# A two-block fp32 network on one core: the pooling layer projects differences of grid rows, and the first modulation moves to TensorE

## The chip, the cores and the metric

One core of a Trainium2 chip runs the whole program as one launch. The metric is the device time of an execution in microseconds (us), as the median of several runs. Five engines work side by side, each through its own instructions in order: TensorE (PE in the profile, with its weight loads as PEld), VectorE (DVE), ScalarE (ACT), GpSimd (POOL) and SyncE (SP), which here only issues transfers. Transfers run on 16 DMA engines.

## The reference, cut to what matters

Two transformer-like blocks run over 256 tokens of width 2048, all in float32. The first block has an even layer and an odd layer.

In every layer a modulation vector comes from the condition: `silu(c) @ w_ada + b_ada`, split into shift, scale and gate. The even layer needs shift and scale for two conditions, `c` for the latent tokens and `c_ctx` for the context tokens. Its input is `u = x * (1 + scale) + shift`, which is projected by `w_in_e`; the first 2048 columns of that projection are the keys and values of both the 256 latent and the 256 context tokens.

The odd layer, here called the pooling layer, is

```
xp, gate = split(u @ w_in_o)                  # 2 x 2048 columns
xg = xp.reshape(4 rows, 64 columns, 2048)     # the 256 tokens are a grid
z  = [mean over a window of rows of g  -  g   for g, window in 4 groups of 512]
z  = (z @ w_pool[group]) * pool_scale
y  = (z * silu(gate)) @ w_out_o
```

The windows are 2, 4, 8 and 16 rows. With 4 rows the last two are the mean over all rows. `z` therefore depends only on differences between grid rows.

The second block holds a recurrent layer (rwkv7) with a bonus term `sum(r * k * r_k)` per head, attention, a cross attention to a memory of 256 tokens, and a feed-forward layer.

## The kernel before, in words

**Products.** Every large projection splits both operands into a high and a low part in a reduced format (`fp32r`) and adds three products: high by high, high by low, low by high. `mm3` (line 162) issues them. Activations stand transposed, 128 input columns by tokens, in tiles `h` and `l`; they are the stationary operand. Weights stream as the moving operand, 512 columns at a time. `load_w` (line 157) fetches two blocks of 128 rows by 512 columns (512 KB) into a `wr` tile, a ring of four, and `split_w` makes `wh` by a ScalarE copy (line 148) and `wl` by a subtraction (line 154), a ring of three each. `split_on` says which engines subtract: (V, G) means that VectorE takes one half and GpSimd the other.

**`project`** (line 182) runs over blocks of 512 output columns, and in each over pairs of 128-row blocks of the weight: one load, then 12 matmuls (two row blocks, two groups of 128 tokens, three products). After each such step it advances the background generator `bg` by `bgn_default` steps. `feed` is a generator advanced in the same places; it makes the input while it is being used.

**Opening.** First the cross attention's keys and values of the memory (`project(memT, ...)`, 16 steps). Behind it, the modulation for the first two blocks of 128 channels is made. Then the channels come in five parts, `PARTS = ((0,2),(2,2),(4,4),(8,4),(12,4))`. Each part transposes its channels of `x` and `ctx`, scales and shifts them (`store_affine`) by the modulation `mod0` of its own channels, and multiplies them with four column blocks of the weight (24 matmuls per load: 4 groups of 128 tokens, two row blocks, three products). The results of the parts are added up in SBUF (lines 528 to 534: ScalarE copies in the first part; in the next two VectorE adds the even ones, and ScalarE and GpSimd the odd ones; VectorE adds all of them later). While a part multiplies, `bg` makes the modulation of the next; `drain` ends it before the next part begins.

Modulation has two forms. `ada_block` streams `w_ada` through TensorE with the four columns `c4` (both conditions, high and low part) as stationary operand. `ada_block_v` multiplies rows of `w_ada` on VectorE (line 355, two conditions, one instruction for each block of 128 rows and condition), from tiles `ar`. In each part, kind 0 (shift) goes by the first and kind 1 (scale) by the second. Both end with small matmuls that bring the result into columns (`pm`): one or two moving columns each.

**Pooling layer** (phase b, lines 972 to 1068). `do_xp(g)` and `do_gate(g)` are projections of 512 columns each from `u1T` (8 steps each); `pool(g)` transposes `xp`, forms the window means minus itself on VectorE, and splits; `mix(g)` multiplies with `w_pool[g]` (2 steps), times `silu(gate)`, and transposes the result. `make_u1` makes `u1T` as the feed of the first projection. `bg` makes the layer's output gate (`ada_gate`: 16 transfers of 256 KB into `ar`, a ring of three, and one VectorE instruction each, line 379) and `affine_x1`, one step for each step of a projection.

**Bonus** (line 1276). Each of 8 pairs of a 128-channel block and a token group is a matmul with the products `qq` as stationary operand and two moving columns.

The program is put in order by a scheduler that starts from the order written and lets an instruction pass one that is not ready, so TensorE's order can differ a little from the text.

Of the kernel before, what the change touches and what calls it, by code (L numbers as in the profile page):

```python
# [17 lines left out]
D = 2048  # L18
# [36 lines left out]
def tile_kernel(ctx: ExitStack, tc: tile.TileContext, I: dict, out: bass.AP):  # L55
# [8 lines left out]
              "b": {"yt": (1024, 8), "h": (512, 8), "f": (512, 8), "gt": (512, 4), "ar": (512, 3), "aa": (512, 1)},  # L64
# [78 lines left out]
    split_on = [(V, G)]  # L143
# [37 lines left out]

    def project(x, w, c0, ncols, evac, korder=None, cw=512, w_k0=0, cbs=None, feed=None, lead=2, late=0, early=0):
# [10 lines left out]
        for cb in cbs:  # L193
# [3 lines left out]
            def products(k0, w, t):  # L197
                for q in range(2):
                    xh, xl = x.get(k0 + q, t)
                    mm3(acc[t][:, :n], xh, xl, w[0][:, q], w[1][:, q], k0 == korder[0] and q == 0,  # L200
                        k0 == korder[-1] and q == 1)
# [41 lines left out]
    def store_affine(x, kt, pt, scale, bias, ts=(0, 1), scratch="h"):  # L243

        full = tl(scratch, [128, 2, T], name="full")
# [8 lines left out]
    def affine_steps(x, src, scale, bias, scratch="h"):  # L254

        for ts, kts in (((0,), (0, 2)), ((1,), (0, 2)), ((0, 1), range(4, 16, 2))):
            for kt in kts:
                store_affine(x, kt, transpose2(src, kt, ts), scale, bias, ts, scratch)
                yield
# [57 lines left out]
    def ada_block(t0, nt, kind):  # L317
# [17 lines left out]
    def set_mod0(pm, t0, nt, kind):  # L335
        b = pr1[:, 32 + kind * 16 + t0:32 + kind * 16 + t0 + nt]
        V.scalar_tensor_tensor(mod0[:, t0:t0 + nt, kind, :], pm, float(kind),
                               b[:, :, None].to_broadcast([128, nt, 2]), op0=AL.add, op1=AL.add)

    def ada_block_v(t0, nt, kind):  # L340
# [17 lines left out]
        pm = pside([128, nt, 2], name="pm")  # L358
        for q in range(nt):
            for a in range(2):  # L360
                PE.matmul(pm[:, q, a:a + 1], acc[a][:, q * 128:(q + 1) * 128], ones[:, :1], start=True, stop=True)
        set_mod0(pm, t0, nt, kind)
# [20 lines left out]
    def ada_cols(l, kind, j):  # L383
        acc = yield from ada_acc(l, kind * D + j * 512)
        pm = pbg([128, 4])
        for q in range(4):
            PE.matmul(pm[:, q:q + 1], acc[:, q * 128:(q + 1) * 128], ones[:, :1], start=True, stop=True)
        c0 = 32 + l * 48 + kind * 16 + j * 4
        V.scalar_tensor_tensor(mod1[:, kind, j * 4:j * 4 + 4], pm, float(kind), pr1[:, c0:c0 + 4], op0=AL.add, op1=AL.add)
# [1456 lines left out]
```

## Time and profile before

| | |
|---|---|
| time, median of 3 runs | 2589.76 us (2586.3 to 2592.92) |
| profiled execution: its own time, its span | 2595.39 us, 2593.7 us |
| TensorE busy in the span | 2442.7 us (94%), 11551 matmuls |
| VectorE, ScalarE, GpSimd busy | 1813.7 us (70%), 1157.8 us (45%), 262.1 us (10%) |
| mean granted TensorE clock | 0.974 |
| transfers | 483.12 MB, mean 186 GB/s |

The opening runs from 0 to about 342 us of the span: the memory's keys and values to 79 us, and then the five parts, whose first matmuls come at 87, 124, 175, 237 and 294 us. The pooling layer begins at 894 us, when its first matmul is issued, and its last transposes end at 1127 us, already among the matmuls of the output projection. The two bonus sums lie at 1341 and 1551 us. A matmul is reported as a record with a modelled end, so neighbouring records overlap; the time that a matmul takes in a stream is read from the distance of the starts. Transposes and matmuls of plain float32 operands appear as two records each.

### The profile page before, as it was taken

The numbers are of one execution on the slowest core, as the hardware profiler recorded it, in microseconds if no ns is written. First come the engines' busy times: TensorE is split into PE (matmuls) and PEld (weight loads), VectorE is DVE, ScalarE is ACT, GpSimd is POOL, SyncE is SP. The second block draws the span as 40 slices with busy tenths as digits, with TensorE's granted clock in tenths as the row PEclk, the third lists the DMA queues.
The fourth block names the chain that finished last, engine by engine and source line by source line (L and its number), as shares of the span: only waits on it lengthen the run. The fifth ranks groups of instructions, "written<-read, shape, count | busy, mean of one in ns | idle before, by whom it ended". The sixth has DMA issues, their size and how long they took to land.

```text
span 2593.7 us, 32574 instructions
## 1 busy us (share of the span) xinstructions
PE 2442.7 (94%) x11551; PEld 1970.2 (76%) x11551; DVE 1813.7 (70%) x2966; ACT 1157.8 (45%) x1542; POOL 262.1 (10%) x233
## 2 busy tenths in 40 slices
PE   7889999899999998999999998999999999999998
PEld 5667767677777787787878777788788888888886
DVE  6789856898898887866778778765655544555544
ACT  5433334343654453444643352255544433444443
POOL 4431000230230000000120121100000000000000
PEclk9889999899999999999999999999999999999999
DMA  7767747667565688755634144145466555666554
GB/s 241 243 196 233 233 130 239 206 225 236 188 219 193 229 268 269 254 189 169 183 109 142 51 138 122 39 146 195 137 181 186 186 187 187 189 184 186 203 187 154
DMA packets 263007, 483.12 MB, mean 186 GB/s; under 512 B 20881, under 2 KB 37099, under 8 KB 262843
## 3 DMA queue, kind: packets, MB, share of 16 engines
q1 hardware_dynamic: 262523, 480.60, 57.8%
q8 instruction: 90, 1.47, 0.2%
q14 instruction: 74, 0.61, 0.1%
q10 hardware_dynamic: 320, 0.44, 0.1%
HBM read 477.82 MB, written 3.15 MB: 185 GB/s over the span
## 4 chain that ended last, share of the span: by engine, by line
PE 54%; DVE 9%; DMA 3%; ACT 2%; issue 2%; POOL 0%; SPq 0%; ACTq 0%; DVEq 0%; POOLq 0%
PE acc L163 15%; PE acc L164 15%; PE acc L165 15%; DVE wl L154 2%; DMA ar<-in_w_ada 2%; PE trp L234 2%; PE pw L1390 1%; ACT wh L148 1%; PE pz L1384 1%; DVE aa L379 1%; DMA wr<-in_w_in 1%; DVE inv L1345 0%; PE pbg L1562 0%; DVE u L1344 0%; DMA lnb<-in_ln_b 0%
## 5 line engine op out<-in xcount | busy, mean ns | idle before, releaser
L148 ACT CAST wh<-wr 128x1024 fp32r<-128x1024 f32 (+2 forms) x720 | 743.9, 1038 | 968.2 <-PE acc L165 830.7
L164 PE MATMUL acc<-wl,xh 128*128 128x512 f32 (+2 forms) x2688 | 1065.5, 396 | 31.2 <-DVE wl L154 30.8
L163 PE MATMUL acc<-wh,xh 128*128 128x512 f32 (+2 forms) x2688 | 1067.6, 398 | 15.4 <-ACT xh L251 6.6
L165 PE MATMUL acc<-wh,xl 128*128 128x512 f32 (+2 forms) x2688 | 1061.7, 396 | 1.9 <-DVE xl L252 1.9
L154 DVE TENSOR_TENSOR wl<-wr,wh 128x512 fp32r<-128x512 f32 (+3 forms) x864 | 587.1, 707 | 168.4 <-ACT wh L148 166.9
L164 PEld LDWEIGHTS acc<-wl,xh 128*128 128x128 f32 x2688 | 514.2, 191 | 152.4 <-DVE wl L154 48.1
L163 PEld LDWEIGHTS acc<-wh,xh 128*128 128x128 f32 x2688 | 512.2, 191 | 129.9 <-ACT xh L251 7.7
L165 PEld LDWEIGHTS acc<-wh,xl 128*128 128x128 f32 x2688 | 513.7, 191 | 110.3 <-DVE xl L252 3.6
L151 DVE TENSOR_TENSOR wl<-wr,wh 128x1024 fp32r<-128x1024 f32 x272 | 333.3, 1225 | 356.4 <-ACT wh L148 356.4
L379 DVE SCALAR_TENSOR_TENSOR aa<-ar,cs,aa 128x512 f32<-128x512 f32 x240 | 190.7, 795 | 74.7 <-DMA ar<-in_w_ada 73.0
L355 DVE SCALAR_TENSOR_TENSOR am<-ar,cs,am 128x512 f32<-128x512 f32 (+1 forms) x150 | 112.4, 794 | 5.7 <-DMA ar<-in_w_ada 5.7
L154 POOL TENSOR_TENSOR wl<-wr,wh 128x512 fp32r<-128x512 f32 (+1 forms) x48 | 66.5, 1400 | 71.7 <-ACT wh L148 71.5
L163 PE MATMUL acc<-wh,uch 128*128 128x512 f32 x128 | 50.0, 392 | 2.5 <-DVE kc L534 2.5
L165 PE MATMUL acc<-wh,ucl 128*128 128x512 f32 x128 | 51.1, 399 | 0.0
L164 PE MATMUL acc<-wl,uch 128*128 128x512 f32 x128 | 51.0, 398 | 0.0
L701 PE MATMUL pp<-eq,ek 128*128 128x128 f32 x224 | 31.2, 294 | 8.8 <-DVE ek L713 8.8
L701 PEld LDWEIGHTS pp<-eq,ek 128*128 128x128 f32 x224 | 30.4, 208 | 11.3 <-issue 8.3
L326 PE MATMUL ada<-wl,c 128*4 128x512 f32 (+1 forms) x80 | 27.6, 356 | 7.9 <-DVE wl L154 7.9
L995 POOL TENSOR_TENSOR sgo<-sgo,psc 128x512 f32<-128x512 f32 x8 | 12.6, 1597 | 191.2 <-ACT sgo L989 134.2
L163 PEld LDWEIGHTS acc<-wh,uch 128*128 128x128 f32 x128 | 24.6, 192 | 8.3 <-DVE kc L534 3.0
L1799 ACT ACTIVATE un<-acc,rml 128x512 f32<-128x512 f32 x32 | 22.0, 688 | 15.6 <-PE acc L165 15.6
L431 DVE SCALAR_TENSOR_TENSOR xl<-trp,pr,xh 128x256 fp32r<-128x256 f32 x48 | 22.4, 480 | 9.4 <-ACT xh L430 9.3
(565 smaller groups left out, 2308.1 us busy)
## 6 DMA issues: line engine op xcount, KB each, us to landing
ar<-in_w_ada SPq DMA_DIRECT2D x320, 256.0 KB
wr<-in_w_in_e SPq DMA_DIRECT2D x128, 512.0 KB
wr<-in_w_up SPq DMA_DIRECT2D x128, 512.0 KB
wr<-in_w_down SPq DMA_DIRECT2D x128, 512.0 KB
wr<-in_w_in SPq DMA_DIRECT2D x80, 512.0 KB
wr<-in_w_in_o SPq DMA_DIRECT2D x64, 512.0 KB
wr<-in_w_ada SPq DMA_DIRECT2D x32, 512.0 KB
wr<-in_w_out_e SPq DMA_DIRECT2D x32, 512.0 KB
```

The source lines that it names most:

```text
L148: S.copy(wh, wr)
L151: engines[0].tensor_tensor(wl, wr, wh.bitcast(F), op=AL.subtract)
L154: engines[q % 2].tensor_tensor(wl[:, q], wr[:, q], wh[:, q].bitcast(F), op=AL.subtract)
L163: PE.matmul(acc, xh, wh, start=start, stop=False)
L164: PE.matmul(acc, xh, wl, start=False, stop=False)
L165: PE.matmul(acc, xl, wh, start=False, stop=stop)
L234: PE.transpose(pt[:, q, t * 128:(t + 1) * 128], src(t, kt + q), ident)
L326: PE.matmul(acc, c4[:, k0 + q], wl[:, q], start=False, stop=k0 + q == 15)
L355: V.scalar_tensor_tensor(acc[a], w[:, q], col, acc[a], op0=AL.mult, op1=AL.add)
L379: V.scalar_tensor_tensor(acc, w, cs[:, k:k + 1], acc, op0=AL.mult, op1=AL.add)
L701: PE.matmul(pp[:, h, t], kx[:, 2 * h + c, s * 128:(s + 1) * 128], qx[:, 2 * h + c, t * 128:(t + 1) * 128], start=c == 0, stop=c == 1)
L1384: PE.matmul(pz[:, i], nt_(i), xt[:, i], start=True, stop=True)
```

## The change

The diff does four things.

1. **First modulation on TensorE.** For parts 0, 1 and 2 a new `ada_both` makes shift and scale of two 128-channel blocks together: 8 loads of 512 KB, each by two transfers of 256 KB, through the rings of the weights, and 32 matmuls of 512 columns. `ada_block_v` remains for parts 3 and 4. From the start on VectorE makes both halves of every `wl`, and VectorE adds all results of the parts after the first.
2. **Differences of grid rows.** `Rows` holds row 1 minus 0 and row 2 minus 1 as 128 tokens (`h`, `l`), and row 3 minus 2 as 64 tokens whose high and low part stand side by side in one tile of 128 columns (`s`). Per 128-row block of the weight the first takes three matmuls, the second two: `s` by the high weights, and the first 64 columns of `s` by the low weights. The two halves of that result are added in `pool`, which forms `z` from the three differences.
3. **Gates first.** The order becomes gates 0, 1, 2, then `xp` 0 and 1, and so on. `make_u1` feeds gate 0 and keeps its unsplit result in `u1n`, from which `rows_of` makes the differences behind gates 1 and 2.
4. **Widened sums.** The small matmuls that bring the modulation into columns stream 128 moving columns (64 pairs for `sel4`) where they streamed one or two, and only the first is used. The bonus sum streams `qq` as moving operand, 256 columns, against 8 stationary columns, four matmuls into one accumulator of 8 rows, which is copied and transposed back.

```diff
-    split_on = [(V, G)]
+    split_on = [(V, V)]
...
+        def products(self, acc, kt, t, wh, wl, start, stop):
+            mm3(acc, *self.get(kt, t), wh, wl, start, stop)
...
-        pm = pside([128, nt, 2], name="pm")
+        pm = pside([128, nt, 64, 2], name="pm")
         for q in range(nt):
-            PE.matmul(pm[:, q], m4[:, q * 128:(q + 1) * 128], sel4, start=True, stop=True)
-        set_mod0(pm, t0, nt, kind)
+            PE.matmul(pm[:, q], m4[:, q * 128:(q + 1) * 128], sel4[:, None, :].to_broadcast([4, 64, 2]), start=True, stop=True)
+        for a in range(2):
+            set_mod0(pm[:, :, 0, a], t0, nt, kind, a)
+
+    def ada_both(t0):
+        acc = pbg([4, 512], "ada")
+        for k0 in range(0, 16, 2):
+            wr = sb.tile([128, 2, 512], F, name="wr", tag="wr", bufs=4)
+            for kind in range(2):
+                c0 = kind * D + t0 * 128
+                nc.sync.dma_start(wr[:, :, kind * 256:kind * 256 + 256],
+                                  ada[0][k0 * 128:(k0 + 2) * 128, c0:c0 + 256].rearrange("(k p) m -> p k m", p=128))
+            wh, wl = split_w(wr, 2, 512)
+            for q in range(2):
+                PE.matmul(acc, c4[:, k0 + q], wh[:, q], start=k0 + q == 0, stop=False)
+                PE.matmul(acc, c4[:, k0 + q], wl[:, q], start=False, stop=k0 + q == 15)
+            yield
+        m4 = tl("h", [4, 512], name="m4")
+        V.tensor_copy(m4, acc)
...
-    bg[0] = together(ada_block_v(*PARTS[0], 1), ada_block(*PARTS[0], 0), mem_scale())
+    bg[0] = together(ada_both(0), mem_scale())
...
-        if j == 2:
-            split_on[0] = (V, V)
...
-        bg[0] = gt_mod() if last else together(ada_block_v(*PARTS[j + 1], 1), ada_block(*PARTS[j + 1], 0))
+        bg[0] = (gt_mod() if last else together(ada_block_v(*PARTS[j + 1], 1), ada_block(*PARTS[j + 1], 0)) if j > 1
+                 else chain(*[ada_both(PARTS[j + 1][0] + q) for q in range(0, PARTS[j + 1][1], 2)]))
...
-                step(2 if last or nt == 2 else 1)
+                step((2, 4, 1, 1, 2)[j])
...
-                elif t % 2 and j < 3:
-                    part = tl("h", name="part")
-                    S.copy(part, acc[t])
-                    G.tensor_tensor(dst, part, dst, op=AL.add)
...
+    class Rows:
+        n = 4
+        def __init__(self):
+            self.h = [tl("xt", [128, 8, 128], R, name="dh") for _ in range(2)]
+            self.l = [tl("xt", [128, 8, 128], R, name="dl") for _ in range(2)]
+            self.s = [tl("dt", [128, 8, 128], R, name="ds") for _ in range(2)]
+
+        def products(self, acc, kt, t, wh, wl, start, stop):
+            p, k = divmod(kt, 8)
+            if t == 0:
+                return mm3(acc, self.h[p][:, k], self.l[p][:, k], wh, wl, start, stop)
+            if start:
+                PE.matmul(acc, self.s[p][:, k], wh, start=True, stop=False)
+            PE.matmul(acc[:64], self.s[p][:, k, :64], wl, start=False, stop=False)
+            if not start:
+                PE.matmul(acc, self.s[p][:, k], wh, start=False, stop=stop)
+
+        def make(self):
+            for kt in range(0, 16, 2):
+                full = u1n[kt // 4][:, kt % 4:kt % 4 + 2]
+                d = tl("h", [128, 2, 192], name="drow")
+                V.tensor_tensor(d, full[:, :, 64:], full[:, :, :192], op=AL.subtract)
+                p, k = divmod(kt, 8)
+                h, l, s_ = [y[p][:, k:k + 2] for y in (self.h, self.l, self.s)]
+                S.copy(h, d[:, :, :128])
+                S.copy(s_[:, :, :64], d[:, :, 128:])
+                yield
+                V.tensor_tensor(l, d[:, :, :128], h.bitcast(F), op=AL.subtract)
+                V.tensor_tensor(s_[:, :, 64:], d[:, :, 128:], s_[:, :, :64].bitcast(F), op=AL.subtract)
+                yield
...
+            V.tensor_tensor(d3, d3, p[:, :, 3], op=AL.add)
...
     def do_xp(g):
-        project(u1T, wo, g * 512, 512, evac_xp(g), feed=None if g else make_u1(), early=0 if g else 2)
+        project(dT, wo, g * 512, 512, evac_xp(g))
...
     def do_gate(g):
-        project(u1T, wo, D + g * 512, 512, evac_gate(g))
+        project(u1T, wo, D + g * 512, 512, evac_gate(g), feed=(make_u1(), rows_of, rows_of, None)[g], lead=0 if g else 2,
+                early=0 if g else 2)
...
+    for g in range(3):
+        do_gate(g)
+    for _ in rows_of:
+        pass
     do_xp(0)
     do_xp(1)
     pool(0)
-    do_gate(0)
+    do_xp(2)
     pool(1)
     mix(0)
-    do_xp(2)
-    do_gate(1)
+    do_xp(3)
+    pool(2)
     mix(1)
-    pool(2)
-    do_xp(3)
-    do_gate(2)
+    do_gate(3)
+    pool(3)
     mix(2)
-    pool(3)
-    do_gate(3)
     mix(3)
...
-                for t in range(2):
-                    PE.matmul(pbon[:, t, 2 * (q + r):2 * (q + r) + 2], qq[:, r, t * 128:(t + 1) * 128], sel2,
-                              start=True, stop=True)
+                c = C_SEL8 + (q + r) * 8
+                PE.matmul(pbon, cst[:, c:c + 8], qq[:, r], start=q + r == 0, stop=q + r == 3)
+        bonT = tl("rp", [8, T], name="bonT")
+        V.tensor_copy(bonT, pbon)
+        pbon = pside([128, 2, 8], name="pbon")
+        for t in range(2):
+            PE.transpose(pbon[:, t], bonT[:, t * 128:(t + 1) * 128], ident[:8, :8])
```

`pool` now has one more addition and forms each group's `z` with 1 (group 0), 8 (group 1) or 6 (groups 2 and 3) VectorE instructions per pair of blocks after it. In `ada_block_v` and `ada_cols` the last matmuls take all 128 columns of `ones`, and `ada_block_v` makes them one condition after the other. The tiles of `zT` move from the `xt` to the `yt` tag, and the last two of `yo` from `yt` to `xt`.

## Rows read from the trace of the kernel before

**Rows 1.** The page's busy times: us, share of the span, instructions.

```profile
PE 2442.7 (94%) x11551; PEld 1970.2 (76%) x11551; DVE 1813.7 (70%) x2966; ACT 1157.8 (45%) x1542; POOL 262.1 (10%) x233
```

**Rows 2.** Stretches of the opening: busy time by engine, clock, transfer share, GB/s.

```profile
12.00:79.00 67.00, 59.00 (x268) 45.63 (x268) 50.58 (x100) 35.80 (x58) 35.59 (x27) 1.00 0.79 253
79.00:124.00 45.00, 36.31 (x162) 27.05 (x161) 34.32 (x57) 22.35 (x34) 15.63 (x13) 0.85 0.75 234
124.00:175.00 51.00, 39.91 (x162) 29.30 (x161) 43.81 (x50) 17.65 (x24) 26.80 (x17) 0.85 0.56 181
175.00:236.00 61.00, 59.88 (x271) 45.85 (x269) 58.60 (x92) 24.45 (x32) 11.88 (x8) 0.96 0.76 246
```

**Rows 3.** What TensorE waited for, 79 to 175 us: total, times, longest.

```profile
PE acc L164 <- DVE wl L154: 7.7, 3, 3.6
PE ada L326 <- DVE wl L154: 5.1, 4, 3.1
PE pm L361 <- DVE am L355: 3.1, 2, 2.9
```

**Rows 4.** VectorE's groups by shape, 124 to 175 us.

```profile
L355 DVE SCALAR_TENSOR_TENSOR am<-ar,cs,am 128x512 f32<-128x512 f32 x22 | 23.9, 1122 | 2.4 <-DMA ar<-in_w_ada 2.4
L154 DVE TENSOR_TENSOR wl<-wr,wh 128x512 fp32r<-128x512 f32 x11 | 12.0, 1095 | 0.0
```

**Rows 5.** VectorE's groups by shape, 236 to 297 us, where GpSimd is idle.

```profile
L154 DVE TENSOR_TENSOR wl<-wr,wh 128x512 fp32r<-128x512 f32 x31 | 20.2, 687 | 0.6 <-ACT wh L148 0.3
L355 DVE SCALAR_TENSOR_TENSOR am<-ar,cs,am 128x512 f32<-128x512 f32 x28 | 19.7, 749 | 0.0
```

**Rows 6.** TensorE in order of time in the opening: start, us, instruction.

```profile
106.97 0.63 PE L165 MATMUL acc<-wh,xl 128*128 128x512 f32 x1
...
111.23 0.63 PE L165 MATMUL acc<-wh,ucl 128*128 128x512 f32 x1
...
120.07 0.95 PE L361 MATMUL pm<-cst,am 128*128 128x1 f32 x8
120.88 1.07 PE L234 MATMUL trp<-cst,xn 128*128 128x128 f32 x8
...
166.78 3.15 PE L361 MATMUL pm<-cst,am 128*128 128x1 f32 x14 [0.18 <-DVE am L355]
```

**Rows 7.** TensorE in order of time, a full stream at the pooling layer's end.

```profile
1111.72 0.39 PE L163 MATMUL acc<-wh,xh 128*128 128x512 f32 x1
...
1124.41 0.39 PE L165 MATMUL acc<-wh,xl 128*128 128x512 f32 x1
```

**Rows 8.** Stretches of the pooling layer, columns as in rows 2.

```profile
920.00:930.00 10.00, 10.00 (x46) 8.29 (x45) 7.22 (x11) 5.13 (x6) 0.00 (x0) 1.00 0.96 325
990.00:1000.00 10.00, 10.00 (x45) 7.98 (x43) 5.48 (x9) 3.72 (x4) 0.00 (x0) 1.00 0.86 300
1030.00:1040.00 10.00, 6.40 (x25) 5.40 (x24) 8.28 (x15) 2.80 (x4) 0.00 (x0) 0.67 0.79 261
898.00:1120.00 222.00, 211.53 (x927) 171.33 (x926) 175.73 (x298) 102.69 (x125) 11.54 (x9) 0.96 0.76 250
```

**Rows 9.** VectorE's groups by shape, 898 to 1120 us.

```profile
L1011 DVE TENSOR_TENSOR rsum<-xpT 128x128 f32<-128x128 f32 x6 | 1.7, 282 | 0.0
...
L1007 DVE TENSOR_TENSOR zT<-xpT 128x384 f32<-128x384 f32 x2 | 1.1, 560 | 1.4 <-ACT xpT L1002 1.4
```

**Rows 10.** What VectorE and TensorE waited for, 898 to 1125 us.

```profile
DVE aa L379 <- DMA ar<-in_w_ada: 17.6, 19, 2.4
...
PE trp L234 <- DVE yo L1035: 8.2, 3, 3.6
```

**Rows 11.** TensorE in order of time around the two bonus sums.

```profile
1340.56 3.58 PE L1276 MATMUL pbon<-cst,qq 128*128 128x2 f32 x16
...
1549.16 1.99 PE L1260 MATMUL pb<-ni,sel8t 8*128 8x256 f32 x8 [0.97 <-DVE ni L1256]
```

**Rows 12.** Stretch around the first bonus sum, columns as in rows 2.

```profile
1338.00:1351.00 13.00, 12.36 (x57) 10.52 (x58) 9.57 (x17) 4.97 (x9) 7.47 (x5) 0.74 0.11 31
```

More of the change, by code (lines that the diff above doesn't have):

```diff
@@ L198, in products @@
                 for q in range(2):
-                    xh, xl = x.get(k0 + q, t)
-                    mm3(acc[t][:, :n], xh, xl, w[0][:, q], w[1][:, q], k0 == korder[0] and q == 0,
-                        k0 == korder[-1] and q == 1)
+                    x.products(acc[t][:, :n], k0 + q, t, w[0][:, q], w[1][:, q], k0 == korder[0] and q == 0,
+                               k0 == korder[-1] and q == 1)
             kept = []
@@ L241, in store_plain, with store_affine @@
         V.tensor_tensor(l, pt, h.bitcast(F), op=AL.subtract)
-    def store_affine(x, kt, pt, scale, bias, ts=(0, 1), scratch="h"):
-        full = tl(scratch, [128, 2, T], name="full")
+    def store_affine(x, kt, pt, scale, bias, ts=(0, 1), scratch="h", full=None):
+        full = tl(scratch, [128, 2, T], name="full") if full is None else full
         s = slice(ts[0] * 128, ts[-1] * 128 + 128)
@@ L357, in ada_block_v @@
                 yield
[L358 to L362, printed above, removed]
+        for a in range(2):
+            pm = pside([128, nt, 128], name="pm")
+            for q in range(nt):
+                PE.matmul(pm[:, q], acc[a][:, q * 128:(q + 1) * 128], ones, start=True, stop=True)
+            set_mod0(pm[:, :, 0], t0, nt, kind, a)
     def together(*gens):
@@ L384, in ada_cols @@
         acc = yield from ada_acc(l, kind * D + j * 512)
-        pm = pbg([128, 4])
+        pm = pbg([128, 4, 128])
         for q in range(4):
-            PE.matmul(pm[:, q:q + 1], acc[:, q * 128:(q + 1) * 128], ones[:, :1], start=True, stop=True)
+            PE.matmul(pm[:, q], acc[:, q * 128:(q + 1) * 128], ones, start=True, stop=True)
         c0 = 32 + l * 48 + kind * 16 + j * 4
-        V.scalar_tensor_tensor(mod1[:, kind, j * 4:j * 4 + 4], pm, float(kind), pr1[:, c0:c0 + 4], op0=AL.add, op1=AL.add)
+        V.scalar_tensor_tensor(mod1[:, kind, j * 4:j * 4 + 4], pm[:, :, 0], float(kind), pr1[:, c0:c0 + 4], op0=AL.add, op1=AL.add)
     gates = {}
@@ L900, in tile_kernel @@
         get = XT.get
+        products = XT.products
     ALPHA = math.sqrt(2.0)
@@ L957, in make_u1 @@
     def make_u1():
[L958 removed]
+        yield from affine_steps(u1T, zcol(x1), lambda k: ab1[:, 1, k:k + 1], lambda k: ab1[:, 0, k:k + 1],
+                                keep=lambda kt: u1n[kt // 4][:, kt % 4:kt % 4 + 2])
     def affine_x1():
@@ L978, in tile_kernel @@
     yoT.n = 4
+    u1n = [tl("yt", [128, 4, T], name="u1n") for _ in range(4)]
+    class Rows:
[26 more added lines that the diff above has]
+                yield
+    dT = Rows()
     def evac_xp(g):
```

60 lines of the change are left out of this document (32 added, 28 removed).

## The prediction

> **What bounds the kernel now.** I read the page's busy times first: TensorE is busy in 94% of the span [rows 1], so over the whole program only fewer matmuls or fewer gaps can help. The change lies in three places, so I read stretches next. In the opening, TensorE is busy 36.3 of 45 us (part 0) and 39.9 of 51 us (part 1), at a mean granted clock of 0.85 in both; in part 2 VectorE is busy 58.6 of 61 us [rows 2]. In the pooling layer TensorE is busy 211.5 of 222 us, VectorE 175.7, and the transfers hold 0.76 of their engines [rows 8]. Then I read the waits of each place: in parts 0 and 1 TensorE waits for VectorE's `wl` and `am` [rows 3]; in the pooling layer VectorE waits 17.6 us in all for `ar`, and TensorE 8.2 us for `yo` [rows 10]. The reader is to see two kinds of place: an opening with gaps, where VectorE is late, and a pooling layer that is a stream of matmuls with two other resources close behind.
>
> **Units.** In a full stream the first and last of 57 matmuls start 12.69 us apart [rows 7]: 12.69 / 56 = 0.227 us for each of 512 columns. In part 0 there is a stretch of 11 matmuls with 4.26 us between first and last start [rows 6]: 0.426 us each, the lower of the clock's two levels (1.2 GHz against 2.4). It follows a wait on `wl` [rows 3].
>
> GpSimd slows VectorE. Beside it, a 512-column `am` takes 1122 ns and a half `wl` 1095 ns [rows 4]; where it is idle they take 749 and 687 [rows 5]. In 51 us that is 22 x 0.373 + 11 x 0.408 = 12.7 us, for 17 GpSimd instructions [rows 2]: about 0.75 us of VectorE for each. A half `wl` that moves from GpSimd to VectorE costs 0.69 and gives back 0.75, so taking GpSimd out costs VectorE nothing.
>
> **Opening, memory stretch** (12 to 79 us). Added: 4 loads' worth of split (8 of 512 KB replace 4, the `ar` transfers go, the bytes stay), and 32 wide matmuls for 32 half as wide, 32 x 0.113 = 3.6 us of TensorE. Removed: the `am` instructions from VectorE, which is busy 50.6 of 67 us. TensorE has 8.0 us of idle there [rows 2], partly the start. Ends: 3.6 us lost, 4.4 gained (8.0 - 3.6). I take 0, as the second half of it is a closed stream.
>
> **Part 0.** Idle is 8.7 us; a clock of 0.85 loses up to 0.15 x 45 = 6.8 us more [rows 2]. Against that stand the same 3.6 us of wider matmuls. So at most 8.7 + 6.8 - 3.6 = 11.9, at least 0. I take 6, half: the two long waits on `wl` behind `am` (which itself waits for `ar`) have no successor, while the chain transpose, scale, split, matmul at the part's start stays.
>
> **Part 1.** Here 64 wide matmuls replace 32 wide ones: 32 x 0.227 = 7.3 us more. Idle is 11.1 us, the clock loses up to 7.7, so at most 11.5 us come back [rows 2]. The small matmuls at its end, 14 in 3.15 us [rows 6], at the lower clock, shrink to the 8 of the other form. VectorE's sum: 20 loads of two halves, 40 x 0.687 = 27.5 [rows 5], 16 additions at about the same 0.69, 11, and some 3.5 for scaling and splitting the inputs: 42 of the 51 us. The transfers' sum: 20 loads of 512 KB and 1 MB of inputs, 11.5 MB, at part 2's 246 GB/s [rows 2] 47 us. With VectorE's 42 and about 4 us for the chain between parts the part takes 46: I take 5 gained. Ends 0 and 11.5.
>
> **Part 2.** 8 additions move to VectorE, 8 x 0.69 = 5.5 us, and 8 GpSimd instructions go, 8 x 0.75 = 6.0. VectorE sets this part's time, so this is 0, within 2 us.
>
> **Widened sums.** In one stretch 8 records with one moving column take 0.95 us and 8 with 128 columns 1.07 [rows 6]: the weight load sets the pace, and widening costs 0.12 us per 8 records, some 2 us in all if nothing came back. What it may bring is the clock over the stretch that follows. In the opening I take 0 for both. The first bonus sum is 16 records in 3.58 us, and 8 records of the new shape (8 rows out, 256 columns; a neighbour with 8 rows in has the same streaming length) take 1.99 [rows 11]. With the copy and the two small transposes I put the new sum at 2.5, so 1.1 us is saved; in the 13 us around it the clock is 0.74 [rows 12], which is worth up to 3.4. I take 2 here and 1 at the second, 3 together; ends -1 (the copy exposed) and 9.
>
> **Pooling layer.** Removed: one of 6 matmuls for each of 4 x 16 row blocks, 64 x 0.227 = 14.5 us. The product of 64 stationary columns still streams 512, so it saves nothing of its own. Added: the rows. Per pair of blocks VectorE subtracts 384, 256 and 128 elements; 128 take 0.28 and 384 take 0.56 [rows 9], 256 between them 0.42: 1.26 us, 8 times 10.1 us, in gates 1 and 2. ScalarE gets 16 small copies; at 102.7 of 222 us [rows 8] it hides them. `pool` loses two instructions in group 0 and gains two in groups 2 and 3 per pair, about 0. VectorE then has 175.7 + 10.1 = 185.8 us, and with the 17.6 of waits [rows 10] 203, in 222 - 14.5 = 207.5. It still fits, with 4 us to spare; I take 1 us of loss. In gates 1 and 2 a step holds two halves of `wl` (1.37), `aa` (0.75, like `am`) and half a row (0.63): 2.75 against 12 x 0.227 = 2.72 of matmuls. Those 16 steps are level, and what is queued behind a late row on VectorE is the next `wl`.
>
> Moved: gates 0 to 2 with their weight loads, their `pool_scale` transfers on SP's queue and their GpSimd products go ahead of `xp`. Their number is the same. The products leave the moment just ahead of each `mix`, where TensorE waits for `yo` [rows 10]; that may bring up to 4 us. At the end, `pool(3)`, `mix(2)`, `mix(3)` now follow each other without a projection between, which may take as much. I take 0 for the pair.
>
> The transfers: an `xp` step moves 512 KB of weights and 256 KB of `ar`, 0.786 MB, in 10 x 0.227 = 2.27 us, if TensorE sets it: 346 GB/s. The fastest of the pooling layer's 10 us stretches moved 325 GB/s with 0.96 of the DMA engines busy, others 300 [rows 8]. At 325 a step takes 2.42 us, and 32 steps lose 4.9 us; at 300 they take 2.62 and lose 11.4; at TensorE's own pace 0. I take 325, the row nearest to what the step asks for.
>
> The Trainium skill (page "SBUF — State Buffer", section "SBUF: two separate sides") gives about 358 GB/s from HBM to a core. By that figure, as an estimate, an `xp` step needs 2.20 us and hides, and the sum would be 4.9 us better. The trace's row differs: its engines are full at 325.
>
> So the pooling layer gains 14.5 - 4.9 - 1 = 8.6; ends 14.5 - 11.4 - 5 = -2 and 14.5 + 4 = 18.5.
>
> **Sum.** 0 + 6 + 5 + 0 + 3 + 8.6 = 22.6 us off the profiled execution's 2595.4 us: 2572.8. The profiled execution is 5.6 us above the median of the runs shown, so for the median 2589.8 - 22.6 = 2567.
>
> **Rivals.**
>
> *Transfers set the pooling layer's pace* (300 GB/s in all `xp` steps). For it: VectorE already waits for `ar`, and these waits grow when a step gets shorter. Against it: between the projections TensorE transposes, and the rings refill. The layer then gains 14.5 - 11.4 - 1 = 2.1, and the time is 2589.8 - 16.1 = 2574.
>
> *The opening does not do what it is changed to.* All modulation now passes through the four `wr` tiles, and every load needs ScalarE's copy, VectorE and a slot. If part 1 keeps its 51 us and part 0 its 45, the time is 2589.8 - 11.6 = 2578. For it: 47 us of transfers in part 1. Against it: TensorE waited there for VectorE, not for a load.
>
> *More comes back.* All idle and lost clock of parts 0 and 1 goes, and the `xp` steps hide: 11.9 + 11.5 + 3 + 13.5 = 40 us, 2550.
>
> *Slower: TensorE starves and its clock falls.* In the pooling layer the clock fell to 0.67 in the one stretch with a wait of 3.6 us [rows 8, 10]. If a starved `xp` step ran at the lower level, it would take 10 x 0.426 = 4.26 us, 2.0 more than counted. All 32 would cost 64 us; from 16 of them on, the change is slower by 16 x 2.0 - 22.6 = 9 us, 2599. Against it: at 300 GB/s a step waits only 0.35 us, and stretches with such short waits show a clock of 1.00 [rows 8].
>
> **How the numbers follow.** The forecast, 2556 to 2578, has 0.55. The first rival has 0.17, the second 0.14, the third 0.09, the slower one 0.05. A measurement of this kernel can tell about 0.3%, 7.8 us, from no change: that is 2582 and 2597.5. The forecast, the third rival and most of the first two lie below 2582; both of the first two together (2589.8 - 5.1) lie within, which I put at 0.09 out of their shares and the forecast's tail. So faster 0.86, same 0.09, slower 0.05. The range 2550 to 2583 takes in the first three rivals.
>
> **What would show it.** In the profile after: no GpSimd work before 340 us except at its start, and `wl` at 0.69 there; part 1 begun by 119 and part 2 by 165 us of the span; clocks of 0.95 or more there; 64 matmuls fewer in the pooling layer, and its stretch some 9 us shorter; `xp` steps between 2.27 and 2.6 us; bonus sums of 8 records in about 2 us. It would be wrong if part 1's steps wait for loads, or if VectorE is busy without a gap through gates 1 and 2 and `xp(0)` starts late behind its rows.

## The result, and the profile after

The changed kernel takes 2557.34 us (median of 4 runs, 2553.56 to 2562.72) against 2589.86 us of the kernel before beside it (4 runs): ratio 0.988, 95% interval 0.9864 to 0.9897, so 32.5 us less. The forecast was 2567, 22.8 us less. The profiled execution took 2557.92 us, its span is 2556.2.

The page's busy times, as in [rows 1]:

```profile
PE 2422.8 (95%) x11491; PEld 1928.6 (75%) x11491; DVE 1796.2 (70%) x2991; ACT 1170.2 (46%) x1560; POOL 172.1 (7%) x169
```

The stretches of the opening, answering to [rows 2] (busy time of TensorE, its weight loads, VectorE, ScalarE, GpSimd; granted clock; transfer share; GB/s):

```profile
12.00:79.00 67.00, 61.77 (x270) 46.09 (x269) 47.20 (x94) 41.54 (x63) 0.00 (x0) 1.00 0.85 284
79.00:124.00 45.00, 41.80 (x174) 28.05 (x175) 36.74 (x63) 26.72 (x38) 0.00 (x0) 0.92 0.82 262
124.00:175.00 51.00, 50.01 (x224) 32.98 (x223) 45.77 (x80) 24.81 (x29) 0.00 (x0) 0.97 0.81 273
175.00:236.00 61.00, 61.00 (x282) 46.77 (x280) 56.43 (x95) 21.62 (x26) 0.00 (x0) 1.00 0.68 212
```

GpSimd is gone, and the clock of 79 to 175 us is up from 0.85 to 0.92 and 0.97. TensorE's waits from 79 to 175 us, answering to [rows 3], and below them VectorE's groups from 124 to 175 us, answering to [rows 4]:

```profile
PE ada L350 <- DVE wl L154: 4.2, 3, 2.9
PE pm L356 <- DVE m L353: 1.9, 2, 1.1
PE acc L163 <- ACT wh L148: 0.2, 1, 0.2
```

```profile
L154 DVE TENSOR_TENSOR wl<-wr,wh 128x512 fp32r<-128x512 f32 x40 | 25.3, 682 | 1.6 <-ACT wh L148 1.6
L381 DVE SCALAR_TENSOR_TENSOR am<-ar,cs,am 128x512 f32<-128x512 f32 x7 | 5.2, 746 | 1.0 <-DMA ar<-in_w_ada 1.0
```

The products `acc` wait for no `wl` any more (7.7 us in [rows 3]); `wl` and `am` are at the durations that [rows 5] showed with GpSimd idle.

The whole pooling layer, from the first transpose of `x1`'s columns to a few us past the last one of `yo`, in the kernel before and in the changed one:

```profile
891.00:1132.00 241.00, 227.91 (x992) 184.06 (x993) 190.42 (x330) 114.45 (x142) 13.04 (x10) 0.96 0.74 246
```

```profile
869.00:1098.00 229.00, 212.13 (x927) 164.85 (x928) 197.07 (x361) 116.95 (x158) 14.94 (x10) 0.97 0.79 260
```

TensorE's longest waits for VectorE in it, before and changed:

```profile
PE trp L234 <- DVE yo L1035: 8.2, 3, 3.6
...
PE acc L164 <- DVE wl L154: 2.1, 4, 1.0
```

```profile
PE trp L236 <- DVE yo L1095: 7.7, 3, 4.3
PE acc L164 <- DVE wl L154: 6.8, 8, 1.7
```

TensorE's busy time has shrunk by 15.8 us and the layer by 12: the wait for `yo` has stayed, and that for `wl` has grown from 2.1 to 6.8 us. The first two `xp` projections, 947 to 988 us:

```profile
947.00:988.00 41.00, 39.36 (x167) 28.78 (x166) 32.76 (x50) 17.30 (x18) 3.45 (x4) 1.00 0.90 302
```

Their 16 steps fill 40.4 us (947.45 to 987.86), 2.53 us each. Nine of the 16 take 2.29 to 2.30 us, the pace of ten matmuls; the time above that lies mostly in a few steps with waits for `wl` (0.64 and 0.89 us) and in the background's own matmuls. So 302 GB/s is the mean that these steps moved, not a rate that held every step back. The first bonus sum, answering to [rows 11], and the stretch around it, answering to [rows 12]:

```profile
1305.44 3.55 PE L1339 MATMUL pbon<-qq,cst 128*8 128x256 f32 x8
```

```profile
1303.00:1316.00 13.00, 12.12 (x58) 7.29 (x59) 11.79 (x20) 5.22 (x10) 8.36 (x5) 0.87 0.11 32
```

Eight records take as long as the sixteen of before; the granted clock from 1305.5 to 1309 us is 0.53, about the lower of the two levels.

### The profile page after: what moved, and what is told of

It reads as the page before. It is cut to its first block, busy times and chain, and to the rows that moved or that the text cites. A ratio compares the mean times of both kernels' runs of the same rounds, so it can differ in the third digit from the quotient of the medians.

```text
span 2556.2 us, 32427 instructions
## 1 busy us (share of the span) xinstructions
PE 2422.8 (95%) x11491; PEld 1928.6 (75%) x11491; DVE 1796.2 (70%) x2991; ACT 1170.2 (46%) x1560; POOL 172.1 (7%) x169
## 4 chain that ended last, share of the span: by engine, by line
PE 61%; DVE 18%; DMA 11%; issue 6%; ACT 3%; POOL 1%; SPq 0%; DVEq 0%; ACTq 0%; POOLq 0%
PE acc L165 17%; PE acc L164 17%; PE acc L163 17%; DMA ar<-in_w_ada 8%; DVE wl L154 6%; DVE aa L405 3%; PE trp L236 2%; ACT wh L148 1%; DMA lnb<-in_ln_b 1%; PE pw L1457 1%; PE pz L1451 1%; DVE u L1411 1%; DVE inv L1412 1%; DMA wr<-in_w_in_e 1%; DMA wr<-in_w_in_o 0%
## 5 line engine op out<-in xcount | busy, mean ns | idle before, releaser
L164 PE MATMUL acc<-wl,xh 128*128 128x512 f32 (+2 forms) x2560 | 1005.5, 393 | 22.9 <-DVE wl L154 22.7
L163 PE MATMUL acc<-wh,xh 128*128 128x512 f32 (+2 forms) x2560 | 1011.8, 396 | 14.1 <-ACT xh L253 6.1
L165 PE MATMUL acc<-wh,xl 128*128 128x512 f32 (+2 forms) x2560 | 1003.5, 393 | 2.4 <-DVE xl L254 1.9
L154 DVE TENSOR_TENSOR wl<-wr,wh 128x512 fp32r<-128x512 f32 (+2 forms) x928 | 622.3, 702 | 176.8 <-ACT wh L148 176.1
L164 PEld LDWEIGHTS acc<-wl,xh 128*128 128x128 f32 x2560 | 485.1, 189 | 135.8 <-DVE wl L154 37.2
L163 PEld LDWEIGHTS acc<-wh,xh 128*128 128x128 f32 x2560 | 484.6, 189 | 127.1 <-ACT wh L148 10.0
L165 PEld LDWEIGHTS acc<-wh,xl 128*128 128x128 f32 x2560 | 484.8, 189 | 106.3 <-issue 4.0
L381 DVE SCALAR_TENSOR_TENSOR am<-ar,cs,am 128x512 f32<-128x512 f32 x60 | 42.6, 746 | 7.3 <-DMA ar<-in_w_ada 7.3
L350 PE MATMUL ada<-wl,c 128*4 128x512 f32 x64 | 26.0, 406 | 4.2 <-DVE wl L154 4.2
L164 PE MATMUL acc<-wl,dh 128*128 128x512 f32 x64 | 26.2, 410 | 3.8 <-DVE wl L154 3.7
```

Of the source, the lines that this page charges most:

```text
L154: engines[q % 2].tensor_tensor(wl[:, q], wr[:, q], wh[:, q].bitcast(F), op=AL.subtract)
L163: PE.matmul(acc, xh, wh, start=start, stop=False)
L164: PE.matmul(acc, xh, wl, start=False, stop=False)
L165: PE.matmul(acc, xl, wh, start=False, stop=stop)
L350: PE.matmul(acc, c4[:, k0 + q], wl[:, q], start=False, stop=k0 + q == 15)
L381: V.scalar_tensor_tensor(acc[a], w[:, q], col, acc[a], op0=AL.mult, op1=AL.add)
```

## The experiments

Times are medians; the ratio is to the kernel before on the same chip. A ratio's gain in us is 2590 x (1 - ratio).

| kernel | us | ratio, 95% interval |
|---|---|---|
| opening_alone | 2583.28 | 0.997, 0.9952 to 0.9989 |
| pooling_alone | 2578.21 | 0.9957, 0.9937 to 0.9976 |
| sums_alone | 2586.15 | 0.999, 0.9967 to 1.0012 |
| order_alone | 2583.22 | 0.9971, 0.9955 to 0.9988 |
| opening_and_pooling | 2565.80 | 0.9906, 0.9885 to 0.9926 |
| opening_and_sums | 2569.02 | 0.9918, 0.9897 to 0.9938 |
| gpsimd_back | 2587.41 | 0.998, 0.9965 to 0.9995 |
| old_modulation | 2557.70 | 0.9872, 0.9851 to 0.9894 |
| gpsimd_out_alone | 2572.51 | 0.9935, 0.9918 to 0.9953 |
| half_background | 2553.74 | 0.9857, 0.9836 to 0.9879 |
| few_transfers | 2544.17 | 0.9827, 0.9807 to 0.9847 |
| both_moves | 2546.69 | 0.9826, 0.9805 to 0.9846 |

One table of the traces carries most readings: where part 0 begins in the span (the first `trp` of `xn`), and how long each part of the opening takes, from its first transpose to that of the next.

| kernel | part 0 begins | part 0 | part 1 | part 2 | part 3 |
|---|---|---|---|---|---|
| before | 78.8 | 42.1 | 50.8 | 59.8 | 59.7 |
| order_alone (opening as before) | 77.9 | 38.3 | 51.0 | 60.3 | 60.8 |
| gpsimd_out_alone | 77.3 | 30.9 | 42.9 | 59.6 | 60.1 |
| opening_alone | 73.9 | 40.1 | 42.6 | 59.6 | 60.0 |
| opening_and_pooling | 74.0 | 38.8 | 42.7 | 59.9 | 60.3 |
| sums_alone | 80.8 | 40.2 | 48.5 | 58.8 | 57.6 |
| changed kernel | 75.7 | 39.7 | 43.0 | 57.9 | 56.6 |
| old_modulation | 73.6 | 30.9 | 41.3 | 58.6 | 57.4 |
| gpsimd_back | 80.9 | 46.3 | 65.9 | 58.8 | 56.3 |

Where the code is the same, parts 1 to 3 repeat within about 1 us and part 0 within 4; differences beyond that are the edit's.

**One part of the change at a time.** opening_alone is the kernel before with these edits:

```diff
-    split_on = [(V, G)]
+    split_on = [(V, V)]
...
-    bg[0] = together(ada_block_v(*PARTS[0], 1), ada_block(*PARTS[0], 0), mem_scale())
+    bg[0] = together(ada_both(0), mem_scale())
...
-                elif t % 2 and j < 3:
-                    part = tl("h", name="part")
-                    S.copy(part, acc[t])
-                    G.tensor_tensor(dst, part, dst, op=AL.add)
```

with `ada_both` in parts 0 and 1 too (its own sums are wide here); pooling_alone has `Rows`, gates first and the new `pool`; sums_alone has the wide `pm` and the new bonus sum.

> The kernel before with the opening's part of the change alone: weights halved on VectorE only, the parts' sums added on VectorE, the modulation of the memory stretch and of parts 0 and 1 computed on TensorE; sums not widened, pooling untouched. Theory: taking GpSimd out of the opening frees VectorE from contention, and VectorE's spare time lets the later parts' modulation run early; then nearly all of the 18 us by which the changed kernel left part 3 earlier shows here, with or without the further 5 us around 455 to 478 us: 18 to 24 us less, 2566 to 2572. Rival: the gain of parts 2 to 4 comes from the widened sums, which keep TensorE's clock up; then only the forecast's 11 us or less show here, about 2579.

> The kernel before with the pooling layer's part of the change alone: gates first, xp projected from differences of grid rows, the pooling sums written on differences. Theory: the pooling layer's gain of about 12 us belongs to this part and does not depend on the opening: 2576 to 2580. Rival: the transfers of the weights set the pace of the xp steps, and the changed kernel's pooling gained only because it entered the layer at another phase of clock and background work; then 4 to 7 us: 2583 to 2586.

> The kernel before with the widened sums alone: the modulation's sums over partitions give 128 columns in place of 1 or 2, and the bonus is summed in one row of 8 and transposed. Theory: only the two bonus sums gain, 2 us each, and the opening gives 0 to 2: 2584 to 2588. Rival: wide sums keep the granted clock up in the opening's parts and around 460 us, and bring the 10 to 15 us that the forecast did not have there: 2572 to 2578.

The pooling layer came as the theory said. The opening alone gave less than it said, the sums by their median what it said. By ratios the three gains are 7.8, 11.1 and 2.6 us, 21.5 in all, against 31.1 for the whole. So pairs were run: opening_and_pooling is the changed kernel with narrow sums (its edit in one of the places below), opening_and_sums the changed kernel with the old pooling layer.

```diff
-            pm = pside([128, nt, 128], name="pm")
...
+        pm = pside([128, nt, 2], name="pm")
...
-                PE.matmul(pm[:, q], acc[a][:, q * 128:(q + 1) * 128], ones, start=True, stop=True)
+                PE.matmul(pm[:, q, a:a + 1], acc[a][:, q * 128:(q + 1) * 128], ones[:, :1], start=True, stop=True)
```

> The changed kernel with the old narrow sums (the modulation's sums over partitions in 1 or 2 columns, except those of the new TensorE modulation, and the old bonus sums). The three parts alone gave 7, 12 and 4 us less, together 23 of the 32 us. Theory: they add up, and what is missing is the scatter of single runs; then this is 2559 to 2565. Rival: the widened sums are worth more beside the new opening than alone, because they come between matmuls that now run closer together; then what was missing is here, and this is 2567 to 2572.

> The changed kernel with the old pooling layer (old order, three full products, old pooling sums). Theory: the pooling layer's part is worth the same 11 to 12 us beside the others as alone: 2567 to 2571. Rival: opening and sums are worth only the 11 us that they gave one by one, and the pooling layer gains more when the opening has run: 2576 to 2580.

The second came out by the theory; the first between the two. Three gains that simply add up, chosen so that they miss the six ratios least (a least squares fit, weighted by the intervals), are opening 11.3 +- 3.6, pooling 12.4 +- 3.5, sums 7.0 +- 3.8 us; they give back all six ratios within their intervals. So an interaction is not needed, and not excluded at a few us.

**What the wide sums do** stands in the table: part 3 takes 56.6 with them and 60.0 without, part 2 57.9 and 59.6. At the end of part 2, opening_and_pooling:

```profile
211.14 1.62 PE L387 MATMUL pm<-cst,am 128*128 128x1 f32 x14
213.70 1.84 PE L334 MATMUL pm<-cst,m 4*128 4x2 f32 x8 [0.94 <-DVE m L331]
215.46 2.82 PE L236 MATMUL trp<-cst,xn 128*128 128x128 f32 x12
```

```profile
211.00:221.00 10.00, 9.04 (x45) 7.29 (x43) 4.91 (x11) 3.37 (x5) 0.00 (x0) 0.66 0.43 130
```

and the changed kernel at the same place:

```profile
213.97 1.28 PE L387 MATMUL pm<-cst,am 128*128 128x128 f32 x10
215.18 1.15 PE L334 MATMUL pm<-cst,m 4*128 4x128 f32 x8
216.26 1.53 PE L236 MATMUL trp<-cst,xn 128*128 128x128 f32 x12
```

```profile
211.00:221.00 10.00, 10.00 (x60) 7.47 (x59) 9.44 (x21) 5.45 (x10) 0.00 (x0) 1.00 0.70 227
```

After matmuls of 1 and 2 columns and a short wait the granted clock is 0.66, the twelve transposes take 2.82 us and the transfers fall to 130 GB/s; after matmuls of 128 columns it is 1.00, 1.53 us and 227 GB/s. Neither half of this is shown to do it alone: in the kernel before, 8 matmuls of one column without a wait were followed by eight transposes in 1.07 us [rows 6], and in the changed kernel the `xp` stretch above keeps its clock of 1.00 through waits of 0.64 and 0.89 us.

**The order alone.**

> The kernel before with the order of the pooling layer alone changed: gates 0 to 2 first, then the xp projections, with three full products each and the old pooling sums. Theory: the order by itself moves the same matmuls about and is worth 0 to 2 us either way, so that the gain of the pooling layer is that of the missing products: 2586 to 2592. Rival: the order fills waits of TensorE on the pooling's own results, and half of the 12 us are due to it: 2582 to 2585.

The rival was right: 7.5 us by the ratio. The layer's length, from the first transpose of `x1`'s columns to the last one of `yo`, is 234.7, 235.1, 231.6, 232.1 and 229.7 us in the five kernels with the old layer (mean 232.6), 225.4 with the new order alone, and 223.3, 220.1, 219.8, 220.1 and 221.4 in five with the new layer (mean 220.9). By these means the order brings 7 of 11.7 us, the missing products and rows together 4.5; the first rests on one profile, and layers of the same kind spread by 3 to 5 us. In order_alone the whole layer and TensorE's largest waits are:

```profile
886.00:1118.00 232.00, 223.13 (x992) 181.23 (x993) 191.72 (x330) 114.42 (x142) 13.30 (x10) 0.97 0.78 256
```

```profile
PE trp L234 <- DVE yo L1035: 6.4, 2, 5.2
PE trp L234 <- DVE z L941: 3.6, 1, 3.6
```

It is idle for 8.9 us (232 - 223.13); the changed kernel, with 64 matmuls fewer, for 16.9 (229 - 212.13). So in this pair TensorE's work shrinks by 11 us, and 8 of them turn up as idle time: the wait for `yo` is still there, and one for `wl` has come (6.8 us). Where the idle time lies, the lengths of the projections tell, each from its first matmul to the next one's. `xp(0)` to `xp(2)` take 68.3 us in order_alone and 60.5 to 62.8 in the five kernels with the new layer, so 6 of the 24 x 2 x 0.227 = 10.9 us of missing products come back there. Gate 2 takes 22.6 us in order_alone, which has no rows to make, and 24.7 to 26.6 in the five; VectorE makes the last rows in its first 2 us. In the changed kernel this gate, and VectorE's and TensorE's waits in it, are:

```profile
920.50:947.30 26.80, 23.74 (x100) 18.25 (x100) 19.65 (x32) 10.55 (x14) 3.75 (x3) 1.00 0.75 247
```

```profile
DVE aa L405 <- DMA ar<-in_w_ada: 6.3, 4, 3.4
```

```profile
PE acc L164 <- DVE wl L154: 3.1, 3, 1.7
```

**GpSimd, and the modulation on TensorE.** gpsimd_back is the changed kernel with this:

```diff
-    split_on = [(V, V)]
+    split_on = [(V, G)]
...
+        if j == 2:
+            split_on[0] = (V, V)
...
+                elif t % 2 and j < 3:
+                    part = tl("h", name="part")
+                    S.copy(part, acc[t])
+                    G.tensor_tensor(dst, part, dst, op=AL.add)
```

> The changed kernel with GpSimd put back into the opening: every second half of a weight tile's difference in the memory stretch and parts 0 and 1, and the odd tiles' sums of parts 1 and 2. Theory: VectorE's contention with GpSimd is what the opening's gain came from: 6 to 12 us more than the changed kernel, 2563 to 2569, with the weight differences back at some 1 us in these stretches. Rival: the gain came from moving the modulation's sums to TensorE, and GpSimd's share of the weight differences was help: 2552 to 2559.

The mechanism was the theory's, its size far above the 6 to 12 us expected: 26 us by the ratios (0.998 - 0.988). VectorE's groups from 124 to 175 us:

```profile
L154 DVE TENSOR_TENSOR wl<-wr,wh 128x512 fp32r<-128x512 f32 x16 | 19.8, 1241 | 2.0 <-ACT wh L148 2.0
L381 DVE SCALAR_TENSOR_TENSOR am<-ar,cs,am 128x512 f32<-128x512 f32 x12 | 15.7, 1318 | 4.4 <-DMA ar<-in_w_ada 4.4
L561 DVE TENSOR_TENSOR kc<-acc,kc 128x512 f32<-128x512 f32 x2 | 1.4, 692 | 2.0 <-PE acc L165 2.0
```

That stretch, GpSimd's largest group from 79 to 190 us, and TensorE's waits from 79 to 195 us:

```profile
124.00:175.00 51.00, 37.57 (x150) 21.85 (x148) 41.80 (x46) 22.36 (x28) 35.87 (x23) 0.93 0.69 219
```

```profile
L154 POOL TENSOR_TENSOR wl<-wr,wh 128x512 fp32r<-128x512 f32 x31 | 51.9, 1697 | 36.9 <-ACT wh L148 28.4 <-PE acc L164 4.6 <-DMA wr<-in_w_in_e 4.0
```

```profile
PE acc L164 <- DVE wl L154: 11.9, 4, 3.9
PE ada L350 <- DVE wl L154: 6.2, 4, 3.1
```

VectorE loses 16 x 0.559 + 12 x 0.572 = 15.8 us beside 23 GpSimd instructions, 0.69 us for each. The Trainium skill (page "SBUF — State Buffer", section "SBUF: two separate sides") says that VectorE and GpSimd share one port pair as an exclusive lock, held for a whole instruction, and that a VectorE operation takes it if it runs in a 2-port mode or, against a GpSimd one that reads SBUF, if both its inputs are in SBUF. The trace agrees: `wl` and `am` have two such inputs and slow down, `kc` reads its other input from PSUM and takes 692 ns as always. It shows the waiting itself: from 12 to 200 us all 36 `wl` and `am` instructions of VectorE that took over 1 us began while a GpSimd instruction ran, and each ended 0.55 us after that one did, however long the two had overlapped. One such pair:

```profile
154.96 1.80 POOL L154 TENSOR_TENSOR wl<-wr,wh 128x512 fp32r<-128x512 f32 x1 [1.54 <-ACT wh L148]
```

```profile
155.87 1.44 DVE L154 TENSOR_TENSOR wl<-wr,wh 128x512 fp32r<-128x512 f32 x1 [0.26 <-ACT wh L148]
```

GpSimd's ends at 156.76 us, VectorE's at 157.31. So VectorE does not run slowly beside GpSimd, it stands still until GpSimd's instruction is over.

old_modulation is the changed kernel with the modulation of before and GpSimd still out:

```diff
-    bg[0] = together(ada_both(0), mem_scale())
+    bg[0] = together(ada_block_v(*PARTS[0], 1), ada_block(*PARTS[0], 0), mem_scale())
...
-                step((2, 4, 1, 1, 2)[j])
+                step(2 if last or nt == 2 else 1)
```

> The changed kernel with the modulation of the memory stretch and of parts 0 and 1 made as before, one half on VectorE and one on TensorE, and GpSimd still left out. Theory: without GpSimd VectorE has the time for its half, which costs it about what the halving of the extra weight tiles costs it in the changed kernel; within 4 us of the changed kernel, 2554 to 2562. Rival: VectorE becomes what TensorE waits for in parts 0 and 1, and the parts go back to their times of before: 2566 to 2572.

The theory's time came, but not for its reason alone: part 0 takes 30.9 us in place of 39.7, and part 4 begins 11 us earlier than in the changed kernel. That lead is 3 us at the pooling layer and 0 at the end. The last single edit took the kernel before and left out GpSimd alone:

```diff
-    split_on = [(V, G)]
+    split_on = [(V, V)]
...
-                elif t % 2 and j < 3:
-                    part = tl("h", name="part")
-                    S.copy(part, acc[t])
-                    G.tensor_tensor(dst, part, dst, op=AL.add)
```

> The kernel before with one edit: GpSimd left out of the opening (weight differences and the parts' sums on VectorE); modulation, sums and pooling as before. Theory: this edit alone is the opening's gain, and the new modulation on TensorE takes part of it back; part 4 begins 25 to 29 us earlier than in the kernel before, and the kernel takes 2566 to 2574. Rival: the lead over the kernel with the new modulation as well (11 us at part 4) is lost again before the end, and the time is that of the opening's part alone, 2579 to 2584.

The theory's time came: 16.8 us by the ratio, more than the whole opening's part (7.8 alone, 11.3 by the fit); part 4 began 20 us earlier than in the profile of before, not 25 to 29. So leaving GpSimd out is the opening's gain, and the modulation on TensorE takes some of it back. The edit takes two things from GpSimd, its halves of `wl` and the parts' sums, and no run separates them; but part 0, where GpSimd adds no sums, takes 30.9 us in place of 38.3 to 42.1.

**The pooling layer's transfers.** half_background is the changed kernel with this:

```diff
+    def every_other(gen):
+        for _ in gen:
+            yield
+            yield
...
     def do_xp(g):
+        rest = bg[0]
+        bg[0] = every_other(rest)
         project(dT, wo, g * 512, 512, evac_xp(g))
+        bg[0] = rest
```

> The changed kernel with the background work (the later layer's modulation: one 128x512 transfer and one VectorE operation a step) stepped only at every second step of the four xp projections; the 16 steps left over run in the output projection behind the pooling layer. Theory: in the xp steps transfers or VectorE set the pace, and this is where the products' saving went that did not show; TensorE's waits on weight differences in the pooling layer, 6.8 us in the changed kernel, fall under 3, and the kernel takes 3 to 5 us less, 2552 to 2555. Rival: the work is only moved, the output projection loses what the xp steps gain; 2556 to 2560.

few_transfers is the changed kernel with this; `once` is set where the pooling layer's background makes the output gates:

```diff
         for k in range(16):
-            w = tl("ar", [128, 512], name="ar")
-            nc.sync.dma_start(w, ada[l][k * 128:(k + 1) * 128, col:col + 512])
+            if k == 0 or not once:
+                w = tl("ar", [128, 512], name="ar")
+                nc.sync.dma_start(w, ada[l][k * 128:(k + 1) * 128, col:col + 512])
```

> The changed kernel with work left out: the background of the pooling layer loads the first of each gate's 16 weight tiles only and multiplies it 16 times, so that VectorE does all its 64 operations and 60 transfers of 256 KB are gone. Theory 1, the transfers set the pace of the xp steps: TensorE's waits on weight differences in the pooling layer fall from 6.8 us to under 2, and the time to 2550 to 2554. Theory 2, VectorE sets it (197 of 226 us busy there): the waits stay at 5 to 7 us, and the time at 2556 to 2560.

With 60 transfers left out the kernel takes 13 us less, more than theory 1 asked. Its pooling layer, 207 us long (223.3 in the changed kernel), TensorE's waits in it, and its gate 2:

```profile
872.00:1086.00 214.00, 207.44 (x931) 163.61 (x932) 197.46 (x362) 118.39 (x159) 14.08 (x10) 0.98 0.66 205
```

```profile
PE acc L164 <- DVE wl L154: 2.2, 2, 1.7
...
PE trp L236 <- DVE yo L1096: 1.9, 2, 1.6
```

```profile
924.00:946.60 22.60, 22.60 (x100) 18.33 (x99) 21.54 (x35) 10.45 (x13) 3.72 (x3) 1.00 0.71 215
```

VectorE does the same 197 us of work in 15 us less, and TensorE's waits for `wl` and `yo` fall from 14.5 us (7.7 + 6.8) to 4.1. In the changed kernel's layer VectorE waits 14.0 us for `ar`, here not at all, and gate 2 takes 22.6 us again, behind the same rows. So VectorE was late because it stood behind `ar`, not because it was full. Half the background in the `xp` steps gave 3.6 us by the medians, as its theory said, though in its profile the waits for `wl` fell to 4.8 us only and not under 3; the intervals overlap, so by itself this is not settled. The output projection that took up the steps stayed a closed stream (74.00 of 74 us busy in both kernels).

**Both edits.**

> The changed kernel with both edits that looked at least as good as it: the modulation of the memory stretch and of parts 0 and 1 as in the kernel before (GpSimd still out), and the background stepped at every second step of the xp projections. Theory: the 11 us lead that the old modulation had at part 4 in one profile is real and was hidden by scatter, and the xp steps give some 3 us more: 2543 to 2551. Rival: the lead is taken back before the pooling layer, as the equal medians of the run with the old modulation say, and only the xp steps count: 2552 to 2557.

2546.69 us: the theory's range. Its interval, 0.9805 to 0.9846, lies below the changed kernel's, so this is the fastest version found, 14 +- 7 us by the ratios (0.988 - 0.9826).

## Why the prediction was right, and where its terms were off

The forecast, its range and its sign held: GpSimd out, narrow sums gone and products saved make it faster by 1.2%. By place the sum was less good than as a whole: parts 0 and 1, the sums of the opening, the bonus sums and two terms of the pooling layer missed in both directions, and that the misses partly cancelled was luck.

- **Memory stretch, 0 taken:** part 0 begins at 73.6 to 77.3 us in the nine kernels with GpSimd out, at 77.3 to 78.8 in the three with the opening as before: 2 to 3 us, inside the bound of 4.4.
- **Part 0, 6 taken: 0 to 2.** GpSimd out would bring it to 30.9 us. `ada_both` brings it back to 39.7. Of these 8.8 us, 3.6 are the wider matmuls that the prediction counted, and in opening_alone TensorE waits 4.2 us for `wl` there against 1.7 in gpsimd_out_alone; the clock makes up the rest (0.72 in the first 10 us of opening_alone's part 0; over the whole part 0.91 in the changed kernel and 1.00 in gpsimd_out_alone, worth up to 0.09 x 39.7 = 3.6 us). How these three overlap is not shown. This was the second rival, in one place: more loads through `wr`, ScalarE and VectorE. Over whole kernels the modulation on TensorE costs 9, 2 and 8 us in three comparisons (gpsimd_out_alone and opening_alone, old_modulation and the changed kernel, both_moves and half_background), each +- 7 to 8, so some 6 +- 4.
- **Part 1, 5 taken: 8.** It begins at 115.4 us and ends at 158.3. All of it is GpSimd: 42.9 us with that edit alone. The price of 0.75 us for a GpSimd instruction was right (0.69); what it leaves out is that TensorE also waits for late `wl` (7.7 us in [rows 3], none in the changed kernel), so that a trade even for VectorE was no even trade for TensorE.
- **Widened sums in the opening, 0 taken: 5**, in parts 2 and 3 beside the new opening (3 to 4 in sums_alone), by the granted clock. This step failed: the prediction saw from [rows 6] that widening is nearly free, and put nothing for the clock behind it, though it put 3 for the same effect in the bonus sums.
- **Bonus sums, 3 taken: none seen.** The new sum takes 3.55 us, not 2.5, because it runs at the lower clock (0.53 from 1305.5 to 1309 us). From the first `pd` (1283.6 us, 1318.7 before) to the transposes behind the layer (1755.7, 1793.9) the changed kernel gains 3.1 us, but over the eight profiles with wide sums that stretch takes 475.6 us on average, over the six with narrow ones 475.9.
- **Pooling layer, 8.6 taken: 12**, from two errors of opposite sign. The order was put at 0 and is worth 7. The products and rows were put at 8.6 and bring 4.5. The price of an `xp` step was nearly right: the first three projections lose 10.9 - 6 = 5 us over 24 steps, 0.2 us each, between the 0.15 taken (2.42 us a step) and the first rival's 0.35 (2.62); most steps run at TensorE's pace. The term that failed is the 1 us for the rows. The prediction added up VectorE's work and its waits for `ar` over the whole layer and found that they fit; but gate 2, right behind the rows, alone loses 2 to 4 us, in waits of up to 3.4 us for one `ar`. It takes both, the rows and the transfers: without the first (order_alone) or the second (few_transfers) gate 2 takes 22.6 us. So the transfers are no ceiling on every step; they cost time through VectorE, which works in order and stands behind a late `ar` with the next `wl` or `yo`. How the rows make `ar` late is not shown. The Trainium skill's figure for HBM to a core (page "SBUF — State Buffer", section "SBUF: two separate sides", about 358 GB/s), by which the steps would hide, was not reached: the fastest 10 us of the changed kernel's pooling layer moved 341 GB/s with 0.97 of the DMA engines busy.

The slower rival did not come: the layer's clock is 0.97. The stretches of [rows 8] that the prediction sets against it hold no wait at all; but the trace of before has others, 1025 to 1030 us with a wait of 0.3 us for one, whose clock is 1.00. Of the marks named ahead, the `xp` steps kept theirs (2.53 us), part 0's clock (0.92) missed 0.95, and the bonus sums missed 2 us.

Left open: why old_modulation's lead at part 4 was gone at its end, where the same edit beside half the background was worth 8 us by the ratios (+- 8), and whether the 2 us of the sums' 7 that parts 2 and 3 do not explain exist.

## What to carry to other kernels

Test a change's parts one by one and in pairs: here one small edit (GpSimd out) was worth more than the part it came with, and an order taken for neutral brought, by one profile, at least as much as the saved products. A helper engine that slows the busy one by as much as it does itself is a loss wherever a third engine waits for the slow results. When matmuls are removed from a step that also loads weights, look for the engine that takes its work in order and has a transfer in that order: it need not be full to be late, and a mean rate over the steps does not show at which of them TensorE waits. Here moving part of the background's transfers elsewhere gave the better version.

## What was not expected of the hardware

- Matmuls of 1 or 2 columns cost more than their own time. Following 14 + 8 of them and a wait of 0.94 us, a stretch of 10 us had a granted clock of 0.66; with 128 columns each and no wait, 1.00. Eight of them, or a wait of about that length, were not followed by this where they stood alone. The wide sums themselves take hardly longer (10 in 1.28 us, against 14 in 1.62).
- While the clock was low, transfers fell too (130 GB/s against 227); that the weights' tiles come free later is the likely reason, and no run tests it.
- Beside GpSimd a VectorE operation with one input in PSUM keeps its 0.69 us, one with both in SBUF takes 1.24 to 1.32 in the mean: where GpSimd began first, it ends 0.55 us behind GpSimd's instruction.
- Single profiles of the same code scatter: from the first `pp` (480.6 us in the kernel before) to the pooling layer, where all kernels of this study run the same code but for wide or narrow sums, the time is 404 to 418 us. A few us between two profiles far from the edit are no evidence.
